# A state read with the state as weights: 128x128 float32 weights and 16 moving columns per stream, in place of 32-column weights and 256 moving columns

## The chip, the cores and the metric

The kernel runs on one core of a Trainium2 chip. The metric is the device time of one execution in microseconds. A core has TensorE (PE in the profile; its weight loads are listed apart as PEld), VectorE (DVE), ScalarE (ACT), GpSimd (POOL) and SyncE (SP), each with an instruction stream of its own, and 16 DMA engines that serve the queues of SP, ACT and POOL.

## What is computed

One layer of a streaming encoder for 256 new tokens of one stream and 16 tokens of each of 8 running streams (384 tokens, width 2048, all float32): a projection, a pooling branch, a Mamba-2 branch, their gated sum, and an MLP. The change lies in the Mamba-2 branch, where each of the 64 heads (8 groups of 8; head dimension 64, state 128) of a running stream has a stored state `h`:

```python
y = jnp.einsum('btsgr,bsgrp->btgrp', cb[..., None] * decay, xdt)
y = y + jnp.einsum('btgn,bgrpn->btgrp', Cc, h) * jnp.exp(cum)[..., None]     # the read of the stored state
h = h * jnp.exp(last)[..., None, None] + jnp.einsum('bsgn,bsgr,bsgrp->bgrpn', Bc, w_end, xdt)
...
y = y + d_skip[..., None] * xh
a_ssd = gated_rmsnorm(y, z, ssd_norm)
```

For the 8 running streams the second line is, per head, a product of 16 rows of `C` with the stream's 128x64 state, and a factor `exp(cum)` per token and head. The new streams start from no state and have no such term.

## The kernel before

**Products.** Large products are made at close to float32 precision: each operand is split into a high part (`wh`, `xgh`) and the rest (`wl`, `xgl`), and three matmuls add up wh.xh, wh.xl and wl.xh (`mm3`, L101 to L103). A weight unit is 128x1024 (512 KB); SyncE's queue fetches it into `w` (L63), ScalarE makes `wh` (L70) and VectorE `wl` (L71), with three buffers each. A projection of 128 channels takes two units, each used by 24 matmuls of 384 columns.

**The Mamba-2 stage.** A loop runs over the 8 groups `g`. A group has ten projections: six with a convolution (`conv`: four `x` tiles, `B` as `BT`, `C` as `CT`; L609 to L626) and four gates `z` (`zproj`). Its 8 heads are two pairs `D.p[0]` and `D.p[1]` (a "pair" `S` has 4 heads, in two tiles of 128 channels, so 16 pairs in all). Between projections stand lumps of small float32 matmuls, chained in TensorE's order by `lump`: `t_pp` (new state of the prompt), `t_cb` (C.B products, once a group), `t_yT` and `t_Y` for one pair, `t_yi` for the next, and the state's update `t_su`. One lump stands after the third `x` projection of a group, one after its last `z`.

**The read of the state before.** `pload` brings a pair's states into `hs`, 128 (state) x 8 streams x 256 (4 heads x 64). `cside` makes from `CT` two masked copies `Cm`, in which either the even or the odd streams' columns are zero. `t_yi` takes, for each 32 tokens (two streams), 32 columns of `Cm` as weights and the stream's 256 columns of `hs` as moving operand, in one of four column strips of the array, and so gets 128 tokens x 256 channels (`yi`). `yside` multiplies each row by its factor (`tok[:, 10]`, one value per token and head) into `yis`. `t_yT` turns `yis` by two transpositions into the tiles `Y` (channels x tokens), into which `t_Y` then adds; `final` reads all 384 columns of `Y`, adds the skip term into `x` and multiplies by `z`.

**The order.** The instructions of an engine are placed by a scheduler that goes by the program's order, by its own estimates of the durations and by the constraints that the code gives (`behind`, `later`, `dve_later`). ScalarE needs one table for `Silu` and another for `Exp`; where the next function needs the other table, an ACT_TABLE_LOAD stands ahead of it.

Of the kernel before, what the change touches and what calls it, by code (L numbers as in the profile page):

```python
# [33 lines left out]
def build(ctx, tc, io):  # L34
# [181 lines left out]
    t_scr = [dram.tile([T, P], F32, name=f"t_scr{i}") for i in range(40)]  # L216
    d_scr = dram.tile([P, NH], F32, name="d_scr")
    cum_scr = dram.tile([NH, T], F32, name="cum_scr")
    dec_scr = dram.tile([NH, NB], F32, name="dec_scr")

    win = io["w_in"]
# [148 lines left out]
    with tc.tile_pool(name="phc", bufs=1, reuse_waits="tile") as pc, tc.tile_pool(name="phc2", bufs=2, reuse_waits="tile") as pc2:  # L370
# [99 lines left out]
        def dt_phase(pb):  # L470
            ps = mmtile("pj_dt")[:, :T]
            for q in range(2):
                w = wpool.tile([P, 1024], F32, tag="w", name=f"w_dt{q}")
                hl = wpool.tile([P, 8, 2, NH], F32R, tag="wh", name=f"wh_dt{q}")
                wv = w[:, :512].rearrange("p (k n) -> p k n", k=8)
                sy.dma_start(w[:, :512], io["w_dt"][q])
                s.activation(hl[:, :, 0], wv, AF.Copy)
                v.tensor_tensor(hl[:, :, 1], wv, hl[:, :, 0].bitcast(F32), ALU.subtract)
                for k in range(8):
                    c = hl[:, k].rearrange("p a n -> p (a n)")  # L480
                    te.matmul(pairs(ps), c, woven(xg[q * 8 + k][0]), start=q + k == 0, stop=False)
# [38 lines left out]
            s.activation(we, we, AF.Exp)  # L520
            v.tensor_tensor(dtw, dt, we, ALU.mult)
            s.activation(nb[:, TP:], cum[:, TP:], AF.Exp)
            dec = pb.tile([NH, NB], F32, name="dec")
            s.activation(dec, last.squeeze(2), AF.Exp)
            sy.dma_start(dec_scr, dec)
            sy.dma_start(decb, dec_scr.partition_broadcast(P))
            srcs = [cum[:, i * P : i * P + P] for i in range(3)] + [dt[:, i * P : i * P + P] for i in range(3)]
            srcs += [dtw[:, i * P : i * P + P] for i in range(3)] + [nb[:, :P], nb[:, TP:]]
            return srcs
# [53 lines left out]
    with tc.tile_pool(name="phd", bufs=2, reuse_waits="tile") as pd, tc.tile_pool(  # L583
# [101 lines left out]
        def cload(S):  # L685
            S.cbcs = []
            for q in range(2):
                cbc = pd.tile([P, 2, T], F32, tag="cbc", name=f"cbc{S.nm}_{q}")
                s.dma_start(cbc, cum_scr[S.h0 + q * 2 : S.h0 + q * 2 + 2, :].partition_broadcast(P))
                S.cbcs.append(cbc)  # L690

        def t_cb(D):
            D.cb = sstile(f"cb{D.g}")
# [5 lines left out]

        def t_yi(S):  # L700
            S.yi = S.py[:, 256:]
            for c in range(4):
                for r in range(2):
                    i = te.matmul(
                        S.yi[c * 32 : c * 32 + 32, :],
                        S.D.Cm[:, r, c * 32 : c * 32 + 32],
                        S.hs[:, 2 * c + r, :],
                        start=r == 0,
                        stop=r == 1,
                    )  # L710
            return i

        def t_yT(S):
            S.Ys = []
            for q in range(2):
                Y = sstile(f"Y{S.nm}_{q}")
                i = te.transpose(Y[:, TP:T], S.yis[:, q], ident)
                S.Ys.append(Y)
            S.Yb = sstile(f"Yb{S.nm}")
            return i  # L720

        lower, upper = slice(0, 64), slice(64, P)

        def t_Y(S):
            for q in range(2):
                Ya, Yb = S.Ys[q], S.Yb[:, q * TP : q * TP + TP]
                for r, sb, e0, n, o, c0 in (
# [7 lines left out]
                    for h in range(2):  # L735
# [1 line left out]
                            o[h * 64 : h * 64 + 64, c0 : c0 + n],  # L737
                            S.xdt[r, q, sb, h * 64 : h * 64 + 64],
                            S.E[r, q * 2 + h, e0 : e0 + n],
                            start=r is upper and q + sb == 0,  # L740
                            stop=sb > 0,
                            skip_group_check=True,
                        )
# [25 lines left out]
                    out=D.Bd[:, 1], in0=D.BD, scalar=sign, in1=D.Bd[:, 0].bitcast(F32), op0=ALU.mult, op1=ALU.subtract  # L769
                )  # L770

        def cside(D):
            D.Cm = pd.tile([P, 2, P], F32, tag="Cm", name=f"Cm{D.g}", bufs=1)
            v.tensor_tensor(
                D.Cm,
                D.CT[:, TP:].unsqueeze(1).to_broadcast([P, 2, P]),
                cst[:, C_CM : C_CM + 256].rearrange("p (a t) -> p a t", a=2),
                ALU.mult,
            )

        def mside(D):
            D.cbm = pd.tile([P, 512], F32, tag="cbm", name=f"cbm{D.g}", bufs=1)
            mask = cst[:, C_MASK : C_MASK + 512]
# [3 lines left out]

        def yside(S):
            S.yis = pd.tile([P, 2, P], F32, tag="yis", name=f"yis{S.nm}", bufs=1)
            S.ready = v.tensor_tensor(  # L790
                S.yis.rearrange("p j (h q) -> p (j h) q", h=2),
                S.yi.rearrange("p (h q) -> p h q", h=4),
                tok[:, 10, S.h0 : S.h0 + 4].unsqueeze(2).to_broadcast([P, 4, 64]),
                ALU.mult,
            )

        def xside(S):
            S.xdt = pd.tile([P, 2, 3, P], F32, tag="xdt", name=f"xdt{S.nm}", bufs=1)
# [59 lines left out]
        def state(S):  # L858
# [18 lines left out]
            lump(t_su)  # L877
            gp.dma_start(io["new_ssm_s"][S.qd], S.hs)

        def final(S):  # L880
            D, g = S.D, S.g
            pe = pd.tile([P, 2, P], F32, tag="pe", name=f"pe{S.nm}", bufs=1)
# [3 lines left out]
                D.ssum = pd.tile([P, T], F32, tag="ssum", name=f"ssum{g}", bufs=1)  # L886
            for q, j in enumerate(S.js):
                x, z = D.xs[j], D.zs[j]
                i = v.scalar_tensor_tensor(
                    out=x,  # L890
                    in0=x,
                    scalar=vec[:, V_DSK + g * 4 + j : V_DSK + g * 4 + j + 1],
                    in1=S.Ys[q][:, :T],
                    op0=ALU.mult,
                    op1=ALU.add,
                )
                if q == 0:
                    S.taken = i
                xm = x[:, 64 : 64 + TP]
# [38 lines left out]
        for g in range(G + 1):  # L938
            if g == G:
# [5 lines left out]
                    [lambda: eside(S, 1)],  # L945
                    [lambda: dside(S)],
                    [lambda: expside(S)],
                    [lambda: fside(S, 0), lambda: fside(S, 1)],
                    [],
                ]  # L950

# [5 lines left out]
                for i in range(4):  # L957
                    gate_b(i, pd, "cacc", between)
                py = mmtile("pp_last")
                lump(lambda: t_yT(prev.p[1]))  # L960
                lump(lambda: t_Y(prev.p[1]))
                lump(lambda: t_pp(prev.p[1], py))
                state(prev.p[1])
# [47 lines left out]
            D.done = silu[0]  # L1011
            if g:
                fside(prev.p[1], 1)
            cside(D)
            b2 = conv_in(u0 + 4, g * 4 + 2)
            S = D.p[0]
            S.py = mmtile(f"py{S.nm}")
# [1 line left out]
                lump(lambda: t_pp(prev.p[1], S.py))  # L1019
            lump(lambda: t_cb(D))  # L1020
            if g:
                lump(lambda: t_yT(prev.p[1]))
                lump(lambda: t_Y(prev.p[1]))
            lump(lambda: t_yi(S))
            mside(D)
# [36 lines left out]
            pload(D.p[1])  # L1062
            fside(S, 0)
            fside(S, 1)
            zproj(2)
            zproj(3)
            S1 = D.p[1]
            S1.py = mmtile(f"py{S1.nm}")
            lump(lambda: t_pp(S, S1.py))
            lump(lambda: t_yT(S))  # L1070
            lump(lambda: t_Y(S))
            lump(lambda: t_yi(S1))
            yside(S1)
# [520 lines left out]
```

## Time and profile before

| | |
|---|---|
| median of 3 runs | 2633.75 us (2633.08 to 2634.02) |
| profiled execution | 2633.2 us, its span 2631.4 us |
| busy: PE, PEld, DVE, ACT, POOL | 2621.3, 2523.4, 1573.0, 1159.7, 368.6 us |
| granted TensorE clock, mean | 0.999 |
| Mamba-2 stage | about 415 to 1155 us of the span |

Busy times are sums over the instructions of an engine. A line of the timeline gives the start, the length, the engine, the line of the code, the operation, the tiles it writes and reads, its shape and how many instructions are put together; in brackets stands the idle time of the engine before it, and what ended that. In a line of groups, the numbers behind the bar are the busy time, the mean length of one in ns, and the idle time before them.

### The profile page before, as it was taken

The numbers are of one execution on the slowest core, as the hardware profiler recorded it, in microseconds if no ns is written. First come the engines' busy times: TensorE is split into PE (matmuls) and PEld (weight loads), VectorE is DVE, ScalarE is ACT, GpSimd is POOL, SyncE is SP. The second block draws the span as 40 slices with busy tenths as digits, with TensorE's granted clock in tenths as the row PEclk, the third lists the DMA queues.
The fourth block names the chain that finished last, engine by engine and source line by source line (L and its number), as shares of the span: only waits on it lengthen the run. The fifth ranks groups of instructions, "written<-read, shape, count | busy, mean of one in ns | idle before, by whom it ended". The sixth has DMA issues, their size and how long they took to land.

```text
span 2631.4 us, 40780 instructions
## 1 busy us (share of the span) xinstructions
PE 2621.3 (100%) x16189; PEld 2523.4 (96%) x16189; DVE 1573.0 (60%) x2286; ACT 1159.7 (44%) x1789; POOL 368.6 (14%) x545
## 2 busy tenths in 40 slices
PE   9999999999999999999999999999999999999998
PEld 9999999999999999999999989999999999989897
DVE  6685335799999999967444436434444444444446
ACT  6443324657565756555333336433333333333233
POOL 0000003245444444411000000000000000000000
PEclk9999999999999999999999999999999999999999
DMA  7445446667676767757545544444444444444443
GB/s 276 150 133 156 148 147 223 201 210 238 224 239 211 235 228 238 233 188 260 165 160 160 195 149 133 144 136 136 134 134 135 136 136 136 136 136 136 135 135 131
DMA packets 134256, 456.33 MB, mean 173 GB/s; under 512 B 20545, under 2 KB 27521, under 8 KB 129073
## 3 DMA queue, kind: packets, MB, share of 16 engines
q1 hardware_dynamic: 103552, 361.44, 43.0%
q0 software_dynamic: 23456, 77.47, 8.5%
q10 hardware_dynamic: 7056, 14.81, 1.8%
q8 instruction: 127, 2.08, 0.3%
q14 instruction: 65, 0.52, 0.1%
HBM read 409.27 MB, written 44.37 MB: 172 GB/s over the span
## 4 chain that ended last, share of the span: by engine, by line
PE 99%; DMA 0%; DVE 0%; ACT 0%; SPq 0%; issue 0%; DVEq 0%
PE pj_up L101 6%; PE pj_up L103 6%; PE pj_up L102 6%; PE wd L156 6%; PE wd L155 6%; PE wd L154 6%; PE pj_x L101 5%; PE pj_x L102 5%; PE pj_x L103 5%; PE pj_sp L102 3%; PE pj_z L103 3%; PE pj_z L102 3%; PE pj_z L101 3%; PE pj_sp L103 3%; PE pj_sp L101 3%; PE pj_gb L101 2%
## 5 line engine op out<-in xcount | busy, mean ns | idle before, releaser
L101 PE MATMUL pj_up<-x1h,wh_up 128*128 128x384 f32 (+1 forms) x1024 | 333.7, 326 | 0.0
L103 PE MATMUL pj_up<-x1h,wl_up 128*128 128x384 f32 (+1 forms) x1024 | 333.4, 326 | 0.0
L102 PE MATMUL pj_up<-x1l,wh_up 128*128 128x384 f32 (+1 forms) x1024 | 333.4, 326 | 0.0
L71 DVE TENSOR_TENSOR wl_wd<-w_wd,wh_wd 128x1024 fp32r<-128x1024 f32 x126 | 154.4, 1225 | 240.3 <-ACT wh_wd L70 240.3
L154 PE MATMUL wd<-wh_wd,hh 128*128 128x512 f32 x756 | 286.5, 379 | 0.0
L155 PE MATMUL wd<-wl_wd,hh 128*128 128x512 f32 x756 | 286.5, 379 | 0.0
L156 PE MATMUL wd<-wh_wd,hl 128*128 128x512 f32 x756 | 286.5, 379 | 0.0
L70 ACT ACTIVATE wh_wd<-w_wd 128x1024 fp32r<-128x1024 f32 x126 | 133.1, 1057 | 321.5 <-PE wd L156 261.0
L70 ACT ACTIVATE wh_up<-w_up 128x1024 fp32r<-128x1024 f32 x126 | 133.1, 1057 | 291.9 <-PE pj_up L102 231.7
L71 DVE TENSOR_TENSOR wl_up<-w_up,wh_up 128x1024 fp32r<-128x1024 f32 x126 | 154.4, 1225 | 178.1 <-ACT wh_up L70 178.0
L101 PE MATMUL pj_x<-xgh,wh_x 128*128 128x384 f32 x768 | 251.9, 328 | 0.0
L102 PE MATMUL pj_x<-xgl,wh_x 128*128 128x384 f32 x768 | 250.4, 326 | 0.0
L103 PE MATMUL pj_x<-xgh,wl_x 128*128 128x384 f32 x768 | 250.4, 326 | 0.0
L102 PEld LDWEIGHTS pj_up<-x1l,wh_up 128*128 128x128 f32 x1024 | 193.6, 189 | 0.2
L101 PEld LDWEIGHTS pj_up<-x1h,wh_up 128*128 128x128 f32 x1024 | 193.6, 189 | 0.2
L103 PEld LDWEIGHTS pj_up<-x1h,wl_up 128*128 128x128 f32 x1024 | 193.6, 189 | 0.0
L101 PE MATMUL pj_z<-xgh,wh_z 128*128 128x384 f32 x512 | 166.9, 326 | 0.0
L102 PE MATMUL pj_z<-xgl,wh_z 128*128 128x384 f32 x512 | 166.9, 326 | 0.0
L103 PE MATMUL pj_z<-xgh,wl_z 128*128 128x384 f32 x512 | 166.9, 326 | 0.0
L101 PE MATMUL pj_sp<-abh,wh_sp 128*128 128x384 f32 x512 | 166.9, 326 | 0.0
L102 PE MATMUL pj_sp<-abl,wh_sp 128*128 128x384 f32 x512 | 166.9, 326 | 0.0
L103 PE MATMUL pj_sp<-abh,wl_sp 128*128 128x384 f32 x512 | 166.9, 326 | 0.0
(351 smaller groups left out, 6373.6 us busy)
## 6 DMA issues: line engine op xcount, KB each, us to landing
w_up<-w_up SPq DMA_DIRECT2D x128, 512.0 KB, 3.5
w_wd<-w_down SPq DMA_DIRECT2D x128, 512.0 KB, 3.5
w_x<-w_in SPq DMA_DIRECT2D x96, 512.0 KB, 3.9
w_z<-w_in SPq DMA_DIRECT2D x64, 512.0 KB, 4.4
w_sp<-w_ssd SPq DMA_DIRECT2D x64, 512.0 KB, 3.5
w_ga<-w_ga SPq DMA_DIRECT2D x32, 512.0 KB, 3.6
w_pp<-w_pp SPq DMA_DIRECT2D x32, 512.0 KB, 3.4
hs<-ssm POOLq DMA_DIRECT2D x16, 1024.0 KB, 6.3
```

The costliest lines, as they stand in the source:

```text
L70: cut[0] = s.activation(h, w, AF.Copy)
L71: cut[1] = v.tensor_tensor(l, w, h.bitcast(F32), ALU.subtract)
L101: te.matmul(out, wh, xh, start=first, stop=False, **how)
L102: te.matmul(out, wh, xl, start=False, stop=False, **how)
L103: return te.matmul(out, wl, xh, start=False, stop=last, **how)
L154: te.matmul(out, mh, vh, start=k == 0 and b != held, stop=False, skip_group_check=b == held)
L155: te.matmul(out, mh, vl, start=False, stop=False, skip_group_check=b == held)
L156: last[0] = te.matmul(out, ml, vh, start=False, stop=k == nk - 1, skip_group_check=b == held)
```

## The change

`t_yi` now takes 128 columns of a stream's state as weights (two heads) and that stream's 16 columns of `CT` as moving operand, for 2 halves x 8 streams, so 16 matmuls per pair, and gets the result as channels x tokens. `Cm` and `cside` go, and so do `t_yT` and its transpositions; `t_Y` starts its own tiles. The factors `exp(cum)` go from the row `nb` to DRAM once (`ec_scr`) and come back per pair as `ecb`, spread over the channels, by two DMA issues on ScalarE's queue in `cload`. `yside` multiplies by them. The new `preside` adds the skip term and `yis` for the 128 columns of the running streams into `x`, on VectorE, and `final` does the skip term only for the 256 prompt columns and adds `Y`'s other 64.

```diff
+    ec_scr = dram.tile([NH, P], F32, name="ec_scr")
...
             s.activation(nb[:, TP:], cum[:, TP:], AF.Exp)
+            sy.dma_start(ec_scr, nb[:, TP:])
...
+            S.ecb = pd.tile([P, 2, P], F32, tag="ecb", name=f"ecb{S.nm}")
+            for h in range(2):
+                s.dma_start(
+                    S.ecb[h * 64 : h * 64 + 64], ec_scr[S.h0 + h : S.h0 + h + 3 : 2, :].partition_broadcast(64)
+                )
...
         def t_yi(S):
             S.yi = S.py[:, 256:]
-            for c in range(4):
-                for r in range(2):
+            for q in range(2):
+                for b in range(NB):
+                    c0 = q * P + b * TS_
                     i = te.matmul(
-                        S.yi[c * 32 : c * 32 + 32, :],
-                        S.D.Cm[:, r, c * 32 : c * 32 + 32],
-                        S.hs[:, 2 * c + r, :],
-                        start=r == 0,
-                        stop=r == 1,
+                        S.yi[:, c0 : c0 + TS_],
+                        S.hs[:, b, q * P : q * P + P],
+                        S.D.CT[:, TP + b * TS_ : TP + b * TS_ + TS_],
+                        start=True,
+                        stop=True,
                     )
...
-        def t_yT(S):
-            S.Ys = []
-            for q in range(2):
-                Y = sstile(f"Y{S.nm}_{q}")
-                i = te.transpose(Y[:, TP:T], S.yis[:, q], ident)
-                S.Ys.append(Y)
...
         def t_Y(S):
+            S.Ys = [sstile(f"Y{S.nm}_{q}") for q in range(2)]
...
-                            start=r is upper and q + sb == 0,
+                            start=sb == 0 and (r is lower or q == 0),
...
-        def cside(D):
...
         def yside(S):
             S.yis = pd.tile([P, 2, P], F32, tag="yis", name=f"yis{S.nm}", bufs=1)
-            S.ready = v.tensor_tensor(
-                S.yis.rearrange("p j (h q) -> p (j h) q", h=2),
-                S.yi.rearrange("p (h q) -> p h q", h=4),
-                tok[:, 10, S.h0 : S.h0 + 4].unsqueeze(2).to_broadcast([P, 4, 64]),
-                ALU.mult,
-            )
+            S.ready = v.tensor_tensor(S.yis.rearrange("p j t -> p (j t)"), S.yi, S.ecb.rearrange("p j t -> p (j t)"), ALU.mult)
...
+        def preside(S):
+            for q, j in enumerate(S.js):
+                x = S.D.xs[j][:, TP:]
+                v.scalar_tensor_tensor(
+                    out=x, in0=x, scalar=dskip(S.g, j), in1=S.yis[:, q], op0=ALU.mult, op1=ALU.add
+                )
...
-                i = v.scalar_tensor_tensor(
-                    out=x,
-                    in0=x,
-                    scalar=vec[:, V_DSK + g * 4 + j : V_DSK + g * 4 + j + 1],
-                    in1=S.Ys[q][:, :T],
-                    op0=ALU.mult,
-                    op1=ALU.add,
-                )
+                xp, xl = x[:, :TP], x[:, TP + 64 :]
+                Y = S.Ys[q]
+                i = v.scalar_tensor_tensor(out=xp, in0=xp, scalar=skip, in1=Y[:, :TP], op0=ALU.mult, op1=ALU.add)
+                v.tensor_tensor(xl, xl, Y[:, TP + 64 : T], ALU.add)
```

`preside` is called behind `fside` of the same pair, for the second pair of a group in the next group, where `cside` stood.

The scheduler places ScalarE's and VectorE's instructions otherwise than before. The place shown is group 3, behind its first lump; in groups 1 to 7 it is the same. `ysq2_3` is the square of the second gated tile of the pair before, `E3_0` the decay factors, `xs14` the third convolved `x` tile, `xhl3_0` and `xd3_0` the split operands of the pair's state update, `wh_z3_0_1` the high part of the second weight unit of the gate `z3_0`. ScalarE before:

```order
L906 ACTIVATE ysq2_3_7701<-zs2_3_7078 128x384
L836 ACTIVATE E3_0_7800<-cbc3_0_1_7358,tok_630 128x128
L70 ACTIVATE wh_z3_0_1_7758<-w_z3_0_1_7756 128x1024
L816 ACTIVATE xhl3_0_7717<-xT3_0_7259 128x512
L820 ACTIVATE xd3_0_7720<-xD3_0_7260 128x512
L845 ACT_TABLE_LOAD
L845 ACTIVATE E3_0_7800<-E3_0_7800 128x2048
```

ScalarE after:

```order
L900 ACTIVATE ysq2_3_7784<-zs2_3_7142 128x384
L832 ACT_TABLE_LOAD
L832 ACTIVATE E3_0_7883<-E3_0_7883 128x2048
L628 ACT_TABLE_LOAD
L628 ACTIVATE xs14_7792<-cacc14_7787,vec_71 128x384
L803 ACTIVATE xhl3_0_7800<-xT3_0_7331 128x512
L807 ACTIVATE xd3_0_7803<-xD3_0_7332 128x512
L70 ACTIVATE wh_z3_0_1_7841<-w_z3_0_1_7839 128x1024
```

`wh_z3_0_1` stood ahead of the `Exp` of `E3_0`, and now stands behind it, behind the `Silu` of `xs14` (before, that stood ahead of `ysq2_3`) and behind a second table load.

VectorE at the same place, before; `yis3_0` is the scaled read of the state, `hs2_1` the sums of the state's update, `zs2_3` the tile whose square `ysq2_3` is:

```order
L790 TENSOR_TENSOR yis3_0_7662<-py3_0_7610,tok_630 128x256
L901 TENSOR_TENSOR zs2_2_7014<-zs2_2_7014,xs10_6661 128x384
L900 TENSOR_TENSOR xs11_6750<-xs11_6750,Yb2_1_7625 128x256
L622 SCALAR_TENSOR_TENSOR cacc14_7704<-cbuf1_4146,vec_71,cacc14_7704 128x384
L874 TENSOR_TENSOR hs2_1_6949<-hs2_1_6949,su2_1_0_7664 128x2x256
...
L901 TENSOR_TENSOR zs2_3_7078<-zs2_3_7078,xs11_6750 128x384
...
L810 TENSOR_TENSOR xD3_0_7260<-xD3_0_7260,tokd_4150 128x512
L71 TENSOR_TENSOR wl_z3_0_1_7759<-w_z3_0_1_7756,wh_z3_0_1_7758 128x1024
L817 TENSOR_TENSOR xhl3_0_7717<-xT3_0_7259,xhl3_0_7717 128x512
```

and after:

```order
L782 TENSOR_TENSOR yis3_0_7743<-py3_0_7685,ecb3_0_7432 128x256
...
L895 TENSOR_TENSOR zs2_3_7142<-zs2_3_7142,xs11_6809 128x384
...
L797 TENSOR_TENSOR xD3_0_7332<-xD3_0_7332,tokd_4152 128x512
L873 SCALAR_TENSOR_TENSOR xs12_7317<-xs12_7317,vec_71,yis3_0_7743 128x128
L873 SCALAR_TENSOR_TENSOR xs13_7521<-xs13_7521,vec_71,yis3_0_7743 128x128
L647 STREAM_TRANSPOSE xb14_7869<-xs14_7792 128x384
L804 TENSOR_TENSOR xhl3_0_7800<-xT3_0_7331,xhl3_0_7800 128x512
L808 SCALAR_TENSOR_TENSOR xd3_0_7803<-xD3_0_7332,vec_71,xd3_0_7803 128x512
L71 TENSOR_TENSOR wl_z3_0_1_7842<-w_z3_0_1_7839,wh_z3_0_1_7841 128x1024
```

`wl_z3_0_1` stood right behind `xD3_0`; now `preside` (L873), the transposition of `xs14`, `xhl3_0` and `xd3_0` stand ahead of it.

More of the change, by code (lines that the diff above doesn't have):

```diff
@@ L701, in t_yi @@
             S.yi = S.py[:, 256:]
-            for c in range(4):
-                for r in range(2):
+            for q in range(2):
+                for b in range(NB):
+                    c0 = q * P + b * TS_
                     i = te.matmul(
-                        S.yi[c * 32 : c * 32 + 32, :],
-                        S.D.Cm[:, r, c * 32 : c * 32 + 32],
-                        S.hs[:, 2 * c + r, :],
-                        start=r == 0,
-                        stop=r == 1,
-                    )
-            return i
-        def t_yT(S):
-            S.Ys = []
-            for q in range(2):
-                Y = sstile(f"Y{S.nm}_{q}")
-                i = te.transpose(Y[:, TP:T], S.yis[:, q], ident)
-                S.Ys.append(Y)
-            S.Yb = sstile(f"Yb{S.nm}")
+                        S.yi[:, c0 : c0 + TS_],
[3 more added lines that the diff above has]
+                        stop=True,
+                    )
             return i
@@ L724, in t_Y @@
         def t_Y(S):
+            S.Ys = [sstile(f"Y{S.nm}_{q}") for q in range(2)]
+            S.Yb = sstile(f"Yb{S.nm}")
             for q in range(2):
@@ L770, in bside @@
                 )
-        def cside(D):
[L773 to L777, printed above, removed]
-                ALU.mult,
-            )
         def mside(D):
@@ L789, in yside @@
             S.yis = pd.tile([P, 2, P], F32, tag="yis", name=f"yis{S.nm}", bufs=1)
-            S.ready = v.tensor_tensor(
-                S.yis.rearrange("p j (h q) -> p (j h) q", h=2),
-                S.yi.rearrange("p (h q) -> p h q", h=4),
-                tok[:, 10, S.h0 : S.h0 + 4].unsqueeze(2).to_broadcast([P, 4, 64]),
-                ALU.mult,
-            )
+            S.ready = v.tensor_tensor(S.yis.rearrange("p j t -> p (j t)"), S.yi, S.ecb.rearrange("p j t -> p (j t)"), ALU.mult)
         def xside(S):
@@ L878, in state, with dskip @@
             gp.dma_start(io["new_ssm_s"][S.qd], S.hs)
+        def dskip(g, j):
+            return vec[:, V_DSK + g * 4 + j : V_DSK + g * 4 + j + 1]
+        def preside(S):
[4 more added lines that the diff above has]
+                )
         def final(S):
@@ L888, in final @@
                 x, z = D.xs[j], D.zs[j]
-                i = v.scalar_tensor_tensor(
-                    out=x,
-                    in0=x,
-                    scalar=vec[:, V_DSK + g * 4 + j : V_DSK + g * 4 + j + 1],
-                    in1=S.Ys[q][:, :T],
-                    op0=ALU.mult,
-                    op1=ALU.add,
-                )
+                skip = dskip(g, j)
+                xp, xl = x[:, :TP], x[:, TP + 64 :]
+                Y = S.Ys[q]
+                i = v.scalar_tensor_tensor(out=xp, in0=xp, scalar=skip, in1=Y[:, :TP], op0=ALU.mult, op1=ALU.add)
+                v.tensor_tensor(xl, xl, Y[:, TP + 64 : T], ALU.add)
                 if q == 0:
@@ L947, in build @@
                     [lambda: expside(S)],
-                    [lambda: fside(S, 0), lambda: fside(S, 1)],
+                    [lambda: fside(S, 0), lambda: fside(S, 1), lambda: preside(S)],
                     [],
@@ L959, in build @@
                 py = mmtile("pp_last")
-                lump(lambda: t_yT(prev.p[1]))
                 lump(lambda: t_Y(prev.p[1]))
@@ L1013, in build @@
                 fside(prev.p[1], 1)
-            cside(D)
+                preside(prev.p[1])
             b2 = conv_in(u0 + 4, g * 4 + 2)
@@ L1021, in build @@
             if g:
-                lump(lambda: t_yT(prev.p[1]))
                 lump(lambda: t_Y(prev.p[1]))
@@ L1064, in build @@
             fside(S, 1)
+            preside(S)
             zproj(2)
@@ L1069, in build @@
             lump(lambda: t_pp(S, S1.py))
-            lump(lambda: t_yT(S))
             lump(lambda: t_Y(S))
```

## The prediction

> **What bounds the kernel now.** I read the page's busy times first, then its chain of work that ended last.
>
> ```profile
> PE 2621.3 (100%) x16189; PEld 2523.4 (96%) x16189; DVE 1573.0 (60%) x2286; ACT 1159.7 (44%) x1789; POOL 368.6 (14%) x545
> ...
> PE 99%; DMA 0%; DVE 0%; ACT 0%; SPq 0%; issue 0%; DVEq 0%
> ```
>
> TensorE is busy for the whole span and is 99% of the chain. So whatever lengthens or shortens its own stream reaches the end one to one, and every other engine matters only where TensorE would have to wait for it. The second view is TensorE's timeline around one of the places that the change touches. Each of the 16 pairs of head groups has one such lump of small matmuls between two projections.
>
> ```profile
> 806.67 0.38 PE L717 MATMUL Y<-cst,yis 128*128 128x128 f32 x2
> 806.98 0.43 PE L736 MATMUL Y<-E,xdt 64*64 64x256 f32 x2
> ...
> 808.46 1.09 PE L704 MATMUL py<-hs,Cm 128*32 128x256 f32 x16
> 809.48 0.72 PE L865 MATMUL su<-xd,Bd 32*128 32x256 f32 x16
> 810.13 0.43 PE L101 MATMUL pj_x<-xgh,wh_x 128*128 128x384 f32 x1
> ```
>
> The first column is the start in us. Two transpositions occupy the stream from 806.67 to 806.98, and the state read `t_yi` from 808.46 to 809.48, 1.02 us. Its 8 matmuls of the code stand as 16 records: a full float32 matmul is run as two, each with its own weight load. They lie in four strips of 32 columns and run side by side.
>
> **The change on TensorE.** It replaces these 8 matmuls (32-column weights, 256 columns moving) by 16 (128x128 weights, 16 columns moving), so by 32 records, each with a load of a full 128x128 float32 weight behind which 16 columns are soon through. No row of before has just that. The nearest is a stretch later on where the moving operand is short as well (128 columns), which shows how fast full loads follow one another.
>
> ```profile
> L1316 PEld LDWEIGHTS pj_up<-x1h,wh_up x8: 190/192/192, 1625.6 to 1627.2; 128*128 128x128 f32 x8
> ...
> L1316 PEld LDWEIGHTS pj_up<-x1h,wl_up x8: 192/192/192, 1625.7 to 1627.3; 128*128 128x128 f32 x8
> ```
>
> ```profile
> 1625.60 0.19 PEld L1316 LDWEIGHTS pj_up<-x1h,wh_up 128*128 128x128 f32 x1
> 1625.71 0.19 PEld L1316 LDWEIGHTS pj_up<-x1h,wl_up 128*128 128x128 f32 x1
> ...
> 1627.39 0.97 PEld L1316 LDWEIGHTS pj_up<-x1l,wh_up 128*128 128x128 f32 x8
> ```
>
> From 1625.60 to 1627.39 there are 16 loads: 1.79 / 16 = 0.112 us each, although one load lasts 0.192 from issue to end. So a load starts before the one ahead of it has ended, and 0.112 is what I take. Below it, the bound is loads that cost nothing, with only the streaming left; above it, loads one after the other at 0.192. I stay at the row, since its weights have the same shape and width. The new state read then takes 32 x 0.112 = 3.58 us, and about 0.1 for the change of array shape behind it: the last of the 16 starts at 808.46 + 1.09 - 0.38 = 809.17, `su` 0.31 later, and three rounds over the strips took 809.17 - 808.46 = 0.71, so one round is some 0.22 and 0.1 is left. That is 3.68 in place of 1.02, +2.66.
>
> The transpositions go: two records 0.38 - 0.27 = 0.11 apart (one lasts 0.27), -0.22 together; the rest of the 0.31 in front of `Y` is again a change of shape, and stays. The `start` flags moved in `t_Y` add no instruction. Net per pair 2.66 - 0.22 = +2.44 us, and x16 = **+39.0 us**. Nothing lies beside this: it is all on the one stream that sets the end.
>
> **What the other engines have to deliver.** Weights are split by ScalarE (`wh`) and VectorE (`wl`), and the order of both engines has changed (shown above). In each group from the second on, the split of the second half of `z_0` now stands behind two table loads, the `Exp` of `E` and the `Silu` of `xs`. These are ScalarE, VectorE and the use on TensorE before, in the lump above, and the mean of a `Silu`:
>
> ```profile
> 816.04 0.51 ACT L906 ACTIVATE ysq<-zs 128x384 f32<-128x384 f32 x1
> 816.46 0.39 ACT L836 ACTIVATE E<-cbc,tok 128x128 f32<-128x128 f32 x1
> 816.75 1.04 ACT L70 ACTIVATE wh_z<-w_z 128x1024 fp32r<-128x1024 f32 x1
> 817.70 0.61 ACT L816 ACTIVATE xhl<-xT 128x512 fp32r<-128x512 f32 x1
> 818.22 0.61 ACT L820 ACTIVATE xd<-xD 128x512 fp32r<-128x512 f32 x1
> 818.85 1.28 ACT L845 ACT_TABLE_LOAD   x1
> 820.14 1.92 ACT L845 ACTIVATE E<-E 128x2048 f32<-128x2048 f32 x1
> ```
>
> ```profile
> 808.72 0.61 DVE L889 SCALAR_TENSOR_TENSOR xs<-xs,vec,Y 128x384 f32<-128x384 f32 x1
> ...
> 811.29 0.42 DVE L790 TENSOR_TENSOR yis<-py,tok 128x256 f32<-128x256 f32 x1
> ...
> 815.34 0.55 DVE L901 TENSOR_TENSOR zs<-zs,xs 128x384 f32<-128x384 f32 x1
> ...
> 818.02 1.22 DVE L71 TENSOR_TENSOR wl_z<-w_z,wh_z 128x1024 fp32r<-128x1024 f32 x1
> ...
> 819.76 1.49 DVE L821 SCALAR_TENSOR_TENSOR xd<-xD,vec,xd 128x512 fp32r<-128x512 f32 x1
> 821.18 0.57 DVE L645 STREAM_TRANSPOSE xb<-xs 128x384 f32<-128x384 f32 x1
> ```
>
> ```profile
> 822.10 0.19 PEld L103 LDWEIGHTS pj_z<-xgh,wl_z 128*128 128x128 f32 x1
> ```
>
> ```profile
> L626 ACT ACTIVATE xs<-cacc,vec 128x384 f32<-128x384 f32 x44 | 27.1, 615 | 49.0 <-DVE cacc L622 48.9
> ```
>
> First VectorE's own sum. 0.55 for 384 columns and 0.42 for 256 make 0.13 for 128. So the 384-column operation of `final`, 0.61, becomes one of 0.48 and a 64-column one of some 0.2; where the next operation does not wait, it starts 0.08 before the end, and the two come out even with the one. `preside` adds two of 0.35, 0.27 each in a row, and eight `Cm` of about 0.42 go: 32 x 0.27 - 8 x 0.34 = +6 us, hidden under 39 us more of TensorE in the same stage, unless a single weight comes late.
>
> Before, `wl` was done at 818.02 + 1.22 = 819.24, and TensorE loaded it first at 822.10: 2.9 us to spare. In the same times after the change: `t_yi` starts 0.22 earlier, at 808.24, and its result is there at 808.24 + 3.58 + 0.17 = 811.99 (a matmul's record ends some 0.17 behind its streaming: 0.38 against 0.22). VectorE comes to `yis` at about 810.6 (2.57 from 808.72 to 811.29; one operation of 0.6 now stands behind it and the rest is 0.13 shorter) and waits 1.4 us there with `zs`, the sums of the state and the rest of `final` queued behind. `yis` starts at 812.05. The second `zs` followed it by 815.34 - 811.29 = 4.05, now by 0.13 more, and ends at 816.8. Then ScalarE: square 0.51, table 1.28, `Exp` 1.92, table 1.28, `Silu` 0.62, `xhl` and `xd` 0.52 each from start to start, and some 0.1 in gaps, gives 823.5 for the start of `wh` and 824.5 for its end. VectorE's `xd` waits for ScalarE's, 823.6, `wl` follows it by 821.18 - 819.76 = 1.42, 825.0, and ends at 826.25. TensorE wants it at 822.10 + 2.44 = 824.54. So a **new wait of 1.7 us** in seven of the eight groups, +12 us; the first group's order keeps `wh` ahead of the `Exp`. Its bounds are none (the cover holds) and 3.5 (each step half a microsecond longer). After it, the next weight, split right behind, is 2 us early again, and in the second lump of a group `wh` stays ahead of the `Exp`.
>
> The rule of the Trainium skill that speaks most against this step is in "ScalarE: Activation LUTs", What ACT_TABLE_LOAD costs: a switch of tables is 1.28 us and a drain of about 1.38 more. The trace does not agree: `Exp` starts at 820.14, right at the table's end (818.85 + 1.28). By the page the two loads would make the wait 4.5 us, and the sum 19 us larger; I go by the row.
>
> The transfers:
>
> ```profile
> 822.64 0.81 ACTq L689 DMA_DIRECT2D cbc<-cum_scr  x2
> ```
>
> ```profile
> w_z<-w_in SPq DMA_DIRECT2D x64, 512.0 KB, 4.4
> ```
>
> Two `ecb` issues per pair hold ScalarE's queue for about 0.8 us, as two of `cbc` do. They stand in the last half of `z` and in the convolutions; weight splits are queued behind them, and TensorE waits for those. ScalarE is 44% busy over the span, so I cost them at nothing; uncovered they would be 16 x 0.8 = 13 us. The buffer of the late weight comes free 7 us later, and the fetch into it (4.4 us) would land near 831, for a use near 837. The one issue on SyncE's queue stands ahead of `dec`, for which that queue waits anyway.
>
> **Sum.** 39.0 + 12 = +51 us on the profiled execution's 2633.2 (span 2631.4 and 1.8 around it), 2684.2; the median of the runs is 0.55 higher, so **2684.8 us**.
>
> **Rivals.** (a) The cover holds: steps behind `yis` run 1.7 us faster than I add up, and only TensorE's own 39.0 remains, 2672.8. For it: I stacked measured pieces in an order that never ran. (b) Faster: full loads are hidden and only 16 columns stream. The state read pays from the point where 32 records take less than 1.02 + 0.22 - 0.10 = 1.14 us, 0.036 each; at 0.02 it would give back 0.5 per pair, 8 us, 2625.7. Against it stands 0.112 for loads with a short stream. (c) Loads do not overlap at all: 0.192 each, 32 x 0.08 = 2.6 more per pair, +41, 2726. Against it stands the same row. (d) The clock falls: in these 3.58 us 16 columns stream 32 times, about an eighth of what fills the array; if the array then ran at half clock for as long again, a pair would lose 1.8 us, 29 in all, 2714.
>
> ```profile
> core 0: 2631.4 us, clock 0.999
> ```
>
> This shows the clock in full all through, but no such stretch is in it. The Trainium skill, "TensorE: Matmul & The Clock Gate", Part 1, has the clock halve after an idle window of about 3.4 us; whether loads count as activity no run here shows. (e) The edit makes no difference that can be measured: no reason for it in the rows.
>
> **How the numbers follow.** Forecast 0.60, (a) 0.22, (c) 0.06, (d) 0.06, (b) 0.02, (e) 0.02, anything else slower 0.02. From 2670 (39 us, a load 5 ns cheaper) to 2698 (a wait of 3.5 us) the range takes in the forecast and (a), 0.8. A measurement of this kernel can tell about 0.2%, 5 us, from no change: slower 0.96, same 0.02, faster 0.02.
>
> **What would show it.** The state read's 32 records some 0.11 apart, 3.6 us a lump; no transpositions; TensorE idle once in each group but the first, ahead of `pj_z` and released by `wl_z` of VectorE, 1 to 2.5 us; granted clock at 1. I am wrong if the records stand 0.05 or 0.19 apart, if the idle time is missing or stands elsewhere, or if the clock drops in the lumps.

## The result and the profile after

The changed kernel takes 2701.45 us (median; 2700.68 to 2705.82 over five executions) against 2633.75 us: 67.7 us more, a ratio of 1.026 with a 95% interval of 1.0245 to 1.0275. The forecast was 2684.8 us and its range ended at 2698. The profiled execution took 2702.2 us, its span 2700.4.

The page's busy times and its chain, as quoted of before:

```profile
PE 2688.2 (100%) x16413; PEld 2598.4 (96%) x16413; DVE 1581.6 (59%) x2342; ACT 1162.7 (43%) x1789; POOL 339.0 (13%) x545
...
PE 97%; DMA 1%; DVE 0%; issue 0%; ACT 0%; ACTq 0%; DVEq 0%; SPq 0%; POOLq 0%
```

TensorE is still busy through the whole span and nearly all of the chain, so the 67 us are more time in its own instructions, not a wait for someone else. The view of waits says the same: these are TensorE's waits from the start of the pair stage to the end (us in total, times, longest), each of them once in the whole run, and none is in front of `pj_z`.

```profile
PE pj_x L101 <- ACT wh_x L70: 0.8, 1, 0.8
PE pj_x L103 <- DVE wl_x L71: 0.7, 1, 0.7
PE pj_gb L103 <- DVE wl_gb L71: 0.5, 1, 0.5
PE su L852 <- DVE xs L890: 0.3, 1, 0.3
```

Now the timeline of TensorE at one lump (start, length, line, operation, tiles, shape, count):

```profile
506.33 3.75 PE L712 MATMUL py<-xs,hs 128*128 128x16 f32 x32
510.00 0.72 PE L852 MATMUL su<-xd,Bd 32*128 32x256 f32 x16
510.65 0.43 PE L101 MATMUL pj_x<-xgh,wh_x 128*128 128x384 f32 x1
510.92 0.38 PE L102 MATMUL pj_x<-xgl,wh_x 128*128 128x384 f32 x1
511.09 0.52 PE L103 MATMUL pj_x<-xgh,wl_x 128*128 128x384 f32 x1
511.41 0.52 PE L101 MATMUL pj_x<-xgh,wh_x 128*128 128x384 f32 x1
...
514.71 0.33 PE L103 MATMUL pj_x<-xgh,wl_x 128*128 128x384 f32 x1
514.87 0.33 PE L101 MATMUL pj_x<-xgh,wh_x 128*128 128x384 f32 x1
```

The new state read runs from 506.33 to the start of `su` at 510.00: 3.67 us, where 3.68 was counted. But about 1 us behind it the projection's matmuls change: a record of the same shape lasts 0.52 instead of 0.33, and the starts stand 0.32 apart (511.09, 511.41) instead of 0.16 (514.71, 514.87). Nobody is waited for; the array is slower. The busy times by windows of time give the granted clock (PEclk, the last column but two) for the state read, the gap behind it, and the two stretches after:

```profile
506.33:510.00 3.67, 3.67 (x39) 3.64 (x32) 1.42 (x5) 1.57 (x5) 0.00 (x0) 1.00 0.48 144
510.00:511.06 1.06, 1.06 (x19) 0.94 (x19) 0.95 (x4) 0.40 (x2) 0.00 (x0) 1.00 0.03 12
511.06:514.47 3.41, 3.41 (x13) 3.41 (x12) 3.41 (x8) 3.41 (x12) 0.00 (x0) 0.50 0.11 38
514.47:517.88 3.41, 3.41 (x23) 3.41 (x22) 3.33 (x7) 3.35 (x5) 1.61 (x2) 1.00 0.64 269
```

From 511.06 to 514.47 the clock is 0.50: a window of 3.413 us in which TensorE does half its work, so 1.707 us are lost. The trace's record of the clock has 16 such windows in the pair stage: one behind each of ten state reads, and two in a row at three more, whose last 0.5 to 1.3 us already fall into the first of the two. Three reads have none. The kernel before has no such window there. 16 x 1.707 = 27.3 us. With the 39.0 us of longer TensorE work that makes 66.3 of the 69.0 us between the two spans. PE's busy time hides this, since a matmul at half clock counts as busy for twice as long; and 0.989 as the mean clock looks like nothing.

### The profile page after: what moved, and what is told of

The parts are those of the page before. It is cut to its first block, busy times and chain, and to the rows that moved or that the text cites. A ratio compares the mean times of both kernels' runs of the same rounds, so it can differ in the third digit from the quotient of the medians.

```text
span 2700.4 us, 41343 instructions
## 1 busy us (share of the span) xinstructions
PE 2688.2 (100%) x16413; PEld 2598.4 (96%) x16413; DVE 1581.6 (59%) x2342; ACT 1162.7 (43%) x1789; POOL 339.0 (13%) x545
## 4 chain that ended last, share of the span: by engine, by line
PE 97%; DMA 1%; DVE 0%; issue 0%; ACT 0%; ACTq 0%; DVEq 0%; SPq 0%; POOLq 0%
PE pj_up L101 6%; PE pj_up L103 6%; PE pj_up L102 6%; PE wd L155 6%; PE wd L154 6%; PE wd L156 6%; PE pj_x L101 5%; PE pj_x L103 5%; PE pj_x L102 5%; PE pj_sp L103 3%; PE pj_sp L102 3%; PE pj_sp L101 3%; PE pj_z L103 3%; PE pj_z L102 3%; PE pj_z L101 3%; PE py L712 2%
## 5 line engine op out<-in xcount | busy, mean ns | idle before, releaser
L101 PE MATMUL pj_x<-xgh,wh_x 128*128 128x384 f32 x768 | 261.4, 340 | 0.8 <-ACT wh_x L70 0.8
L103 PE MATMUL pj_x<-xgh,wl_x 128*128 128x384 f32 x768 | 257.8, 336 | 0.7 <-DVE wl_x L71 0.7
L102 PE MATMUL pj_x<-xgl,wh_x 128*128 128x384 f32 x768 | 258.2, 336 | 0.0
```

Of the source, the lines that this page charges most:

```text
L101: te.matmul(out, wh, xh, start=first, stop=False, **how)
L102: te.matmul(out, wh, xl, start=False, stop=False, **how)
L103: return te.matmul(out, wl, xh, start=False, stop=last, **how)
```

## The experiments

Two theories. **Clock**: the 16 windows at half clock are the missing part, and they come because 16 moving columns behind a full load keep the array too little occupied. **Order**: the late weight half costs more than the forecast's 12 us, in a form that does not show as a wait. All times are medians; the kernel before took 2634.0 beside them.

### ScalarE's order put back

```diff
-        cut[0] = s.activation(h, w, AF.Copy)
+        whs[name] = cut[0] = s.activation(h, w, AF.Copy)
...
+            with behind(whs[f"z{g}_0_1"]) if g else behind(S.split):   # ahead of expside(S)
```

> The changed kernel with one thing put back: ScalarE forms the heavy half of the first z unit's second part (wh_z of groups 1 to 7) ahead of the group's Exp again, as the kernel before did, so that the wait which the prediction counted at 12 us cannot arise. TensorE's own instructions stay those of the changed kernel. Theory of the clock (the 67.7 us are 39 us of longer TensorE work and 16 windows of 3.413 us at a clock of 0.5, each 1.707 us, together 27.3 us): the windows stay, 2698 to 2702 us, granted clock 0.99. Theory of the order (the late weight half costs some 12 to 27 us in whatever form): the time falls by as much, to 2674 to 2690 us.

2704.8 us (2703.6 to 2705.6), ratio 1.0269 [1.0253, 1.0284]. Nothing came back, so the order theory falls. The record of the clock has 19 windows instead of 16, 5.1 us more; the span grew by 3.4, so the order itself can have given back no more than some 2 us.

### Wider products over the same loads

```diff
-                        S.yi[:, c0 : c0 + TS_],
+                        S.yi[:, c0 : c0 + min(W, P - b * TS_)],      # W = 32, 64, 128
...
-                        S.D.CT[:, TP + b * TS_ : TP + b * TS_ + TS_],
+                        S.D.CT[:, TP + b * TS_ : TP + b * TS_ + min(W, P - b * TS_)],
```

> The same 32 loads of stored states per chunk pair, but each product moves 32 columns of C instead of 16 (the last of each pass 16); the next product writes over the additional columns, so the result is the same. Mean moved columns 30 instead of 16; by the 0.112 us from load to load the stretch keeps its 3.6 us, and the additional columns lie beside the next load. The order on ScalarE is that of the first experiment. Theory that the clock follows how much TensorE streams: the share of a load's 0.112 us in which columns move rises from some 12 to some 22 per cent; if that is enough, no window at 0.5 and 2633.75 + 39 = 2673 us; if not, 2700 us as before. Theory that the clock follows the loads (their count or their back-to-back order): 2700 us whatever the width.

> As the one before with 64 columns (mean 52, some 39 per cent of a load's 0.112 us). Theory of the streaming share: fewer or no windows at 0.5, 2673 us when there are none, each that is left adds 1.7 us. Theory of the loads: 2700 us.

> As the one before with all columns that are left to the right (128 down to 16, mean 72, some 54 per cent of a load's 0.112 us). Theory of the streaming share: no windows, granted clock 1, 2672 to 2675 us: the 39 us of longer TensorE work stay, the 27 us go. Theory of the loads: 16 windows as in the changed kernel, 2700 us. If the wider products lengthen the stretch itself, its rows stand further apart than 0.112 us and the time is above 2675 us with a clock of 1.

| columns | time | ratio to before, 95% | windows at half clock in the pair stage |
|---|---|---|---|
| 16 (first experiment) | 2704.8 us | 1.0269 [1.0253, 1.0284] | 19 |
| up to 32 | 2700.5 us | 1.0252 [1.0237, 1.0268] | 15 |
| up to 64 | 2676.4 us | 1.0160 [1.0143, 1.0177] | 1 |
| up to 128 | 2675.5 us | 1.0158 [1.0143, 1.0173] | 1, ahead of the first state read |

The same loads, up to eight times the columns (the last product of each pass still has 16), and the kernel is 29 us *faster*. ScalarE's order is not quite held, though the expectations say so: no edit pins it in these three runs. With 32 columns the trace shows the changed kernel's order (`wh_z` behind both table loads), with 64 and 128 it has `wh_z` ahead of the `Exp`, as in the first experiment. That the order is not what keeps the clock up is shown by two runs further down, which have 128 columns and `wh_z` behind both table loads and no window behind a read either.

The stretch itself costs the same; this is the timeline of TensorE at a lump of the last of the four, and the windows of time for it and the 3.4 us behind it:

```profile
738.83 3.75 PE L712 MATMUL py<-xs,hs 128*128 128x128 f32 x32
742.51 0.72 PE L852 MATMUL su<-xd,Bd 32*128 32x256 f32 x16
```

```profile
738.83:742.50 3.67, 3.67 (x40) 3.65 (x32) 3.62 (x11) 2.26 (x7) 0.13 (x2) 1.00 0.63 195
742.50:745.90 3.40, 3.40 (x34) 3.27 (x34) 3.40 (x7) 3.15 (x11) 2.11 (x2) 1.00 0.14 42
```

738.83 to 742.51 is 3.68 us, as with 16 columns: the loads set the pace, and the additional columns run beside them. The clock stays at 1.00 behind it. The span is 2674.6; without its one window (1.7 us) it is 41.5 above before, of which 39.0 are the state read and the transpositions as counted. What is left is the size of the few single waits at the stage's start. With the same 32 loads in a row, the number of moving columns decides on the clock, and the step lies between 32 and 64.

### The wait that the forecast counted

The changed kernel shows no wait in front of `pj_z`. Was it never there, or hidden? The next two runs keep the clock at 1 with the 128 columns and pin ScalarE to the order of the changed kernel.

```diff
+        with behind(hold.get(name)):                     # wh_z of the unit: behind xhl's first half (xd follows that)
             cut[0] = s.activation(h, w, AF.Copy)
...
+            with behind(ex):                             # the Silu behind the Exp
                 silu[0] = s.activation(o, a, AF.Silu, bias=vec[:, V_CB + c : V_CB + c + 1])
```

> The fourth experiment (full-width products, clock at 1) with ScalarE's order pinned as in the changed kernel: in groups 1 to 7 the heavy half of the first z unit's second part stands behind both Exp and both Silu steps again. It asks whether the wait that the prediction counted, and that the changed kernel does not show, is there once the clock stays at 1. In the changed kernel the light half is ready 20.7 us after the stretch begins and TensorE comes to it at 21.2 us, of which 1.7 us are the window at 0.5; without it TensorE comes at 19.5 us, so it should wait 1.2 us, seven times: 8 us above the fourth experiment, 2683 to 2684 us, and idle time of some 1.2 us in front of pj_z. Rival (the wait was never there, whatever the clock): no idle time, 2675 us.

2675.1 us (2673.7 to 2677.0): no wait. But this run does not decide. The light half was ready 0.15 us ahead of TensorE's load, because ScalarE came to the table load ahead of the `Exp` 10.9 us after the lump's start and not 12.3 us as in the changed kernel. There, this stands in front of it:

```profile
654.65 0.37 ACT L880 COPY pe<-py 128x256 f32<-128x256 f32 x1 [2.50 <-DVE yis L782]
655.12 0.53 ACT L900 ACTIVATE ysq<-zs 128x384 f32<-128x384 f32 x1
...
655.57 3.33 ACT L823 ACTIVATE E<-cbc,tok 128x128 f32<-128x128 f32 x11
```

The copy `pe` reads the bank in which the state read stands, and waits 2.50 us until VectorE has been there with `yis`; eleven of the group's sixteen `E` steps are held up behind it. My pins had let those go first. The next run pins these as well, and VectorE's `zs` behind `yis`.

```diff
+                    with behind(pin):                    # E 6 to 16: behind the copy pe; pe: behind E 5
+                        S.lastE = s.activation(
...
+                with behind(rdy if q == 0 else (S.added if rdy else None)):   # zs behind yis, behind hs
                     v.tensor_tensor(z, z, x, ALU.mult)
```

> The fifth experiment again, since there ScalarE came to the first Exp 10.9 us after the stretch group began and not 12.3 us as in the changed kernel: the copy of the state tile and eleven of the sixteen Relu stood in another order. Here they too are pinned as in the changed kernel, and VectorE's products in front of them; full-width products keep the clock at 1. If the predicted wait is real and only hidden by the slow window, the light half of the first z unit's second part is ready some 20.5 us after the start and TensorE comes at 19.5 us: 0.8 to 1.2 us of waiting in seven groups, 6 to 8 us above the fourth experiment, 2681 to 2684 us, with TensorE's idle time in front of pj_z. Rival (no wait at any clock): 2675 us and light halves ready ahead of TensorE.

2684.7 us (2684.3 to 2685.7), 9.2 us above the fourth experiment, and no window at half clock in the pair stage. The waits of TensorE now begin with this one (us in total, times, longest), and the timeline of one group has it in front of the first use of the light half:

```profile
PE pj_z L105 <- DVE wl_z L73: 5.8, 9, 0.9
```

```profile
756.79 0.33 PE L104 MATMUL pj_z<-xgl,wh_z 128*128 128x384 f32 x1
757.78 0.43 PE L105 MATMUL pj_z<-xgh,wl_z 128*128 128x384 f32 x1 [0.67 <-DVE wl_z L73]
```

```profile
757.78 0.19 PEld L105 LDWEIGHTS pj_z<-xgh,wl_z 128*128 128x128 f32 x1 [0.96 <-DVE wl_z L73]
```

The starts of two matmuls stand 0.99 apart instead of 0.16, and the weight load sat idle for 0.96 until VectorE was done. It happens in each of the seven groups, and in two of them a second time in the unit behind. So the wait is real, about 1 us where 1.7 was worked out. (The table load still comes a little early here, 8.92 us behind the start of the read against 9.16 in the changed kernel.) The wait is gone in the changed kernel because the clock is low just then. There the same group looks like this:

```profile
659.57 1.28 ACT L832 ACT_TABLE_LOAD   x1
660.87 1.92 ACT L832 ACTIVATE E<-E 128x2048 f32<-128x2048 f32 x1
662.80 1.28 ACT L628 ACT_TABLE_LOAD   x1
...
665.66 1.05 ACT L70 ACTIVATE wh_z<-w_z 128x1024 fp32r<-128x1024 f32 x1
```

```profile
665.87 0.75 DVE L808 SCALAR_TENSOR_TENSOR xd<-xD,vec,xd 128x512 fp32r<-128x512 f32 x1
666.75 1.23 DVE L71 TENSOR_TENSOR wl_z<-w_z,wh_z 128x1024 fp32r<-128x1024 f32 x1
```

```profile
668.33 0.19 PEld L103 LDWEIGHTS pj_z<-xgh,wl_z 128*128 128x128 f32 x1
```

The order is the feared one, table, `Exp`, table, ..., `wh_z`, and the light half ends at 667.98. But TensorE comes to it only at 668.33, since 1.7 us of that group went into the window at half clock: 0.35 us to spare, where without the window it would have come some 1.3 us too early. All seven of these reads have such a window behind them; the three reads without one are others.

### Two short stretches in place of a long one

```diff
-        def t_yi(S):
+        def t_yi(S, qs=(0, 1)):
...
-            for q in range(2):
+            for q in qs:
...
+            lump(lambda: t_yi(S, (0,)))
             if g:
                 lump(lambda: t_Y(prev.p[1]))
-            lump(lambda: t_yi(S))
+            lump(lambda: t_yi(S, (1,)))              # the same in the group's second lump
```

> The 32 products with 16 columns as in the changed kernel, but the 16 for the first half of the channels stand ahead of the products t_Y and the 16 for the second half behind them: two stretches of 1.8 us instead of one of 3.6 us, the same loads and columns. ScalarE's order is that of the first experiment. In the changed kernel a window at 0.5 followed only where 2.0 us or more of a stretch lay in the window of 3.413 us before it (1.94 us gave none). Theory of the quiet share of a window: no part of 1.8 us reaches that, so few or no windows at 0.5, 2672 to 2677 us (some 0.1 us more per pair for the second entry into the loads). Theory that the clock falls with the number of loads in some longer time: 2700 us as before.

2674.2 us (2672.6 to 2675.6), ratio 1.0154 [1.0139, 1.0169]; no window at half clock behind a state read. The same 32 loads with the same 16 columns cost no clock when 1.5 us of other matmuls lie between their halves. That holds for 15 of the 16 reads. The first has no `t_Y` to part its halves; the grid of windows cuts it into 2.20 and 1.29 us, and no window at half clock followed it.

### The stretch twice as long

```diff
-            for q in range(2):
+            for q in (0, 1, 0, 1):
```

> The 32 loads with 16 columns are carried out twice in a row (the second time writes the same result again), ScalarE's order as in the first experiment: one stretch of 7.2 us. The loads cost 32 x 0.112 us x 16 = 57 us. Theory that each window of 3.413 us filled with such loads is followed by one at 0.5: two or three such windows per stretch instead of one, 27 to 54 us more on top, 2785 to 2815 us. Rival (one window at 0.5 for each stretch, however long): the same 27 to 32 us as in the first experiment, 2762 us.

2811.1 us (2808.9 to 2813.1). The record of the clock has 50 windows at 0.5 (85 us), about three for each of the 16 stretches, in rows of two to four. One such row by windows of time, with 3 us on either side of it, and the timeline's line of its stretch:

```profile
735.00:738.00 3.00, 3.00 (x28) 3.00 (x28) 1.80 (x5) 1.39 (x4) 1.14 (x2) 0.96 0.88 289
737.77:748.01 10.24, 10.24 (x56) 9.98 (x56) 3.82 (x9) 3.23 (x11) 0.54 (x1) 0.50 0.16 47
748.01:751.00 2.99, 2.99 (x20) 2.99 (x19) 2.99 (x6) 1.09 (x3) 2.19 (x3) 1.00 0.93 357
```

```profile
733.86 10.29 PE L713 MATMUL py<-xs,hs 128*128 128x16 f32 x64
```

64 loads at 0.112 would take 7.2 us; here they take 10.2, because the clock falls in the middle of them and the loads then start 0.213 us apart, where they stood 0.112 apart before. So a low clock lengthens the stretch, and more of it lies in the next window.

### Fewer loads

```diff
-                for b in range(NB):
+                for b in range(0, NB, 2):               # 16 loads; the other run: range(1), 4 loads
...
-                        S.yi[:, c0 : c0 + TS_],
+                        S.yi[:, c0 : c0 + 2 * TS_],     # 32 columns; the other run: P, so 128
...
-                        S.D.CT[:, TP + b * TS_ : TP + b * TS_ + TS_],
+                        S.D.CT[:, TP + b * TS_ : TP + b * TS_ + 2 * TS_],
```

Both kernels leave out a part of the state read: the first reads only every second stream's state and uses it for two streams, the other only the first stream's.

> Leaves out half of the carried part: only the eight even streams of each pass, with 32 columns, so that the odd streams are given their neighbour's state; 16 loads instead of 32. By the price of a load (0.112 us each, no cover) the stretch is 1.79 us and the pair costs 2.44 - 1.79 = 0.65 us more than before, 16 pairs 10.4 us: 2644 us, and with the 2 us that the fourth experiment leaves over 2646 us. A stretch of 1.8 us is under the share at which a window followed: clock 1. Rival (the clock falls at any such stretch): some 14 windows more, 24 us, 2668 us.

> Leaves out nearly all of the carried part: one product of 128 columns for each half of the channels, with the first stream's state for all; 2 loads instead of 32. It asks whether everything else in the change (the broadcast transfers, the missing transpositions, the multiplications that moved, the other order) is free. If it is, the pair takes 2.44 - 30 x 0.112 = -0.92 us against before, 16 pairs -14.7 us: 2619 us, up to 2622 us with what the fourth experiment leaves over. If the rest costs something of its own (transfers that come late, ScalarE or VectorE in front of TensorE), the time is above 2625 us and idle time of TensorE shows where.

With 16 loads: 2647.5 us (2646.0 to 2649.4), as expected, clock 1. Against the fourth experiment's span without its one window (2672.9), the span of 2645.5 is 27.4 us shorter for 256 loads: 0.107 us each. (The products here have 32 columns, so this run changes the columns as well as the loads.)

The other run came to 2636.7 us (2634.1 to 2640.7), ratio 1.0011 [1.0002, 1.0021], where 2619 to 2622 was expected. A part of the gap is a miscount in the expectation: two products are four loads, since each float32 matmul has two. By its own working, with 28 loads fewer and not 30, a pair takes 2.44 - 28 x 0.112 = -0.70 us against before, and the time is 2622.6 us, up to 2625. The rest of the change is not free once the loads are gone. TensorE at one lump, in the timeline:

```profile
808.18 0.71 PE L712 MATMUL py<-xs,hs 128*128 128x128 f32 x4
808.83 0.38 PE L852 MATMUL su<-xd,Bd 32*128 32x256 f32 x3
809.42 0.68 PE L852 MATMUL su<-xd,Bd 32*128 32x256 f32 x13 [0.21 <-DVE xs L890]
```

Two things. The four records take 0.65 us up to `su`, where four loads and the 0.1 for the change of array shape make 0.55: 0.1 x 16 = 1.6 us. What the 0.1 more is stays open. And `su` now waits for VectorE, which must first empty `Y` (`xs`, L890) to free its bank; by the starts it takes 1.20 us to the next projection (808.83 to 810.03), not 0.65, and 0.81 in the other lump of a group: 8 x (0.55 + 0.16) = 6 us. With all 32 loads in front of it and the clock at 1, `su` takes 0.65. These 8 us and the 2 to 3 us of single waits are most of the 11.5 between 2622.6 and the profiled execution, which was the fastest of ten (2634.1); what makes the others longer no trace shows. Even with nearly all loads left out, nothing was won, so no version of this state read that beats the kernel before was in sight, and none was run.

## Why the prediction was wrong

**The state read: right.** 32 records, 0.11 apart, 3.67 us a lump where 3.68 was counted; in the runs at full clock TensorE's own 39.0 us were there with 2 to 3 us beside them. The row of full loads from another stage carried over to loads with 16 columns behind them. Rivals (b) and (c), loads hidden or not overlapped at all, fall with it.

**The clock: the step that failed.** Rival (d), "the clock falls", had a chance of 0.06, and the last part set "granted clock at 1" as the sign of being right. Its price came out close, 29 us worked out against 27.3 by the trace's record of the clock, but partly by luck: it took one loss for each of 16 reads, and three reads had none while three had two windows. Its chance was wrong. I had the share that streams ("about an eighth") and the length (3.6 us), and took a clock of 0.999 for evidence, while saying that no such stretch was in that trace. A row that cannot show a thing says nothing against it. What the runs showed in its place: 16 windows at half clock, 27.3 us, gone when the products are wider or the stretch is parted. The Trainium skill, "TensorE: Matmul & The Clock Gate", Part 1, has the clock halve after an idle window of about 3.4 us, and gives 3413 ns for a window that runs free of the kernel; the windows here have just that length and a fixed grid. It leaves open whether weight loads count as activity. These runs say that 32 loads in a row with 16 or 32 columns each do not count as enough.

**The wait: right in mechanism, smaller, and hidden.** Seven waits of 1.7 us, 12 us in all, were forecast. At full clock and in nearly the same order the wait is there, about 1 us in seven groups and 9.2 us in the median. TensorE came when it was said to (16.30 us behind the start of the read by the forecast, 16.29 in the fifth experiment); one step ahead of the light half was costed too long: VectorE's `xd` took 0.75 us (665.87, above), not the 1.49 of the row of before. In the changed kernel the wait is absent, which is what rival (a), "the cover holds", said, but for another reason.

**How they combine.** I made (d) 2714 by adding the clock to the forecast, wait included. But a slower TensorE comes later to the weight, so the clock loss pays for the wait: 2633.75 + 39.0 + 27.3 = 2700.1, and 2701.45 was measured. The run with the wait and without the clock loss came to 2684.7, next to the forecast's 2684.8. That is partly luck: its wait was smaller than forecast, and 2 to 3 us of single waits that the forecast left out made up for it. No sum of mine had the clock loss without the wait.

**The other parts held.** The two transpositions gave back what was counted; the broadcast transfers, ScalarE's `ecb` issues and VectorE's additional work caused no wait of TensorE that shows. That holds only under the cover of the loads: with four of them left, `su` waits for VectorE.

## What to carry to other kernels

Before replacing few wide matmuls by many narrow ones, work out two numbers for the new stretch: how long it lasts by its weight loads, and for what share of that time columns stream. If it lasts for most of a clock window (here 2.4 of 3.41 us was always enough) and streams little, count half a window lost behind it, and break the stretch up or widen its products, which cost nothing here, where the loads set the pace. And two losses that meet at the same place are not added: whatever delays the engine that sets the end gives time to everything that it would have waited for.

## What the runs showed of the hardware

- The windows of the clock lie on a grid of 3.413 us that does not start with the stretch. By the traces' records, a window at full clock was always followed by one at 0.5 when 2.36 us or more of it lay in an unbroken state read with 16 columns, and never when it was 1.99 us or less. Between these there is no sharp bound: 2.08 and 2.12 us brought one, 2.20 us (the first read of the run with two short stretches) did not. With up to 32 columns 2.14 us brought none and 2.33 us one. With up to 64, one of 16 state reads brought one.
- A window that is itself at 0.5 needs less: in the changed kernel 0.47 us of a state read in it (from 941.14 on) was followed by a second one.
- At half clock weight loads are slower too: 0.213 us from start to start instead of 0.112.
- The loss nearly locks onto the loop: in the changed kernel a pair with its lost half window takes 47.9 us (eight pairs from 506.33 to 889.57), close to 14 windows of the grid (47.79), and ten of the windows at half clock in a row start 47.79 us apart.
- Products over the same weight loads were widened from 16 to up to 128 columns (72 in the mean) at no cost: 3.67 and 3.68 us for 32 loads.
- A table load of 1.28 us is followed by its function with no more than 0.02 us between (659.57 + 1.28 to 660.87).
